# One encoder layer on one core: four edits to what stands where in the engines' queues, and TensorE's order in the last attention stage taken from the program text

## The chip, the cores and the metric

The kernel runs on one core of one Trainium2 chip. The metric is the device time of one launch in microseconds (us). The engines are named as the profile names them: PE is TensorE (matmuls and transposes), DVE is VectorE, ACT is ScalarE, POOL is GpSimd, SP is SyncE, which here only issues DMAs. Each engine works through its own queue in order; an instruction that waits for a semaphore holds up all that stands behind it on that engine.

## What is computed

One layer of a bidirectional encoder on 1024 positions of 1024 channels, in float32: a SwiGLU block, a mixer (Fourier branch and differential attention side by side, gated and merged), a second SwiGLU block, a norm.

```python
x = x + 0.5 * swiglu(rms_norm(x, ffn1_norm[l]), ffn1_wg[l], ffn1_wu[l], ffn1_wd[l])
x = x + hybrid_mixer(rms_norm(x, mix_norm[l]), positions, rel_bias, w_in[l], ...)
x = x + 0.5 * swiglu(rms_norm(x, ffn2_norm[l]), ffn2_wg[l], ffn2_wu[l], ffn2_wd[l])
...
# hybrid_mixer
proj = h @ w_in
u_f, q, k, v, g_a, g_b = jnp.split(proj, cuts, axis=-1)
y_a = fourier_branch(u_f) @ w_fourier_out          # real part of a 2-D DFT, 4 groups of 128 channels
o = diff_attention(q, k, v, positions, rel_bias, lam)   # softmax(s1) - lam * softmax(s2), 4 heads
o = rms_norm(o, subln_g, SUBLN_EPS) * (1.0 - lambda_init)
merged = jax.nn.sigmoid(g_a) * y_a + jax.nn.sigmoid(g_b) * (o.reshape(B, S, V_WIDTH) @ w_attn_out)
return merged @ w_out
```

## The kernel before

**Arithmetic.** Each float32 product is taken as three matmuls on halves: an operand is split into a high part (ACT copies it, L133) and a low part (DVE subtracts, L134), and high·high, high·low and low·high are summed in PSUM. The large products (both SwiGLU blocks, the projection by w_in) go by seven products of 2x2 blocks instead of eight; these are the matmuls of L386, twelve to a product and bank, with ACT (L398) and DVE (L402) taking the products out of PSUM.

**Stages.** SwiGLU 1 runs to about 600 us of the span, the projections with the first two heads of attention beside them to about 1115 us, the last attention stage (heads 2 and 3, with the Fourier branch) to about 1262 us, the product with w_attn_out (L1784, called y_b) and the merge with w_out to about 1470 us, SwiGLU 2 and the last norm to the end.

**What sets the order.** The program is traced once; a scheduler that simulates the engines then sets each engine's order, so an instruction need not stand where the text has it. `in_order(...)` pins one instruction behind everything traced before it on its engine. Side work is written as Python generators (`third`, `hgen`, `fgen`), of which a step is traced at each hook of a main loop.

**What the change touches.**
- `ffn` (SwiGLU 1) works on column pairs j, about 37.5 us each; at its hooks it steps `third`, the generator `mixer_weights` (L746), which prepares the mixer's weights: it loads a piece into an `h` tile (L797 for w_attn_out), some steps later splits it on ACT and DVE (L759, L760, pinned), and stores it as `attn_d` (L802).
- `head_prep(h)` (L1232) prepares a head's operands from `proj_d`: `twice` (L1209) loads a half of q or k into an `rh` tile (two DMAs, L1213; the `rh` ring has three buffers), ACT copies the high part (`q_split` L1221, `k_split` L1229), POOL subtracts the low part (L1222, L1230); then V is loaded (L1248), transposed on PE (L1251) and split. Loads and splits of one step are traced together.
- `fourier` (L1403) is traced in steps from `fill(g, k)`: `tokens(j)` loads a group's token rows (L1427), `fold_tokens` folds them on POOL (L1434 to L1440), PE transposes the fold (L1482), ACT and DVE split it, PE multiplies by the DFT matrix (L1509).
- `fetch_op` (L1622) loads eight pieces of `attn_d`, 512 KB each, for y_b; it issues on SP's queue.
- The last attention stage is the loop over query blocks g = 18 to 33 at L1742: `combine(g-1)` (ACT, POOL L1303: the difference of the two softmaxes), `scores(g, 0)` and `scores(g, 1)` (PE L1285, the two score maps, into tiles A), `fill(g, 0)`, at odd g `weigh(g-3)` (PE L1332, the weights times V), a step of `hgen` (`head_prep(3)`, later norms), `fill(g, 1)`, at odd g `back(g-3)` (PE L1343), `turn(g-1)` (PE L1319, the transposes of the weights). Between scores and turn of a block stand DVE's maximum (L1288), ACT's exponentials (L1291), and `combine`.

## Time and profile before

| | us |
|---|---|
| median of three runs | 2056.62 |
| the three runs | 2057.92, 2055.22, 2056.62 |
| the profiled execution, its own time | 2060.26 |
| its span in the trace | 2058.5 |
| PE busy in it | 1959.3 (95%) |

The span is what the profiler sees between the first and the last instruction; 1.8 us of the execution's time lie around it. A row of the timeline gives start, duration, engine, line, operation, output<-input, how many instructions were merged (x12), and in brackets how long the engine sat idle before it and what ended that idleness. A row of stretches gives, for each engine, its busy time and its instructions in that stretch, then the clock that PE was granted (1.00 is the upper of its two levels, 2.4 GHz), the busy share of the 16 DMA engines and what they moved.

### The profile page before, as it was taken

Reading aid. Unit: us, or ns where it says so; the run is one execution under the profiler, and the core shown is the slowest. Engines: PE = TensorE matmul, PEld = TensorE weight load, DVE = VectorE, ACT = ScalarE, POOL = GpSimd, SP = SyncE. Lnnn points to the kernel's source line nnn. Section 1 sums busy time; section 2 is a strip of 40 time slices with the busy share of each in tenths; the row PEclk is TensorE's granted clock in tenths of the full one; section 3 lists DMA queues with packets and bytes.
Section 4 is the critical chain, followed back from the end, with each engine's and each line's share of the span. In section 5 each row is a group of like instructions: output and inputs, shape, how many; then the busy total and the mean of one; then the engine's idle time right before and its main releaser. Section 6 shows DMA issues by size and latency. Waiting matters only on the chain. (4 is left out here: it accounts for less than half of the span.)

```text
span 2058.5 us, 27602 instructions
## 1 busy us (share of the span) xinstructions
PE 1959.3 (95%) x9433; PEld 1640.7 (80%) x9433; DVE 1417.7 (69%) x2152; ACT 1008.5 (49%) x1814; POOL 652.0 (32%) x487
## 2 busy tenths in 40 slices
PE   4999999999999989999999897997999999999998
PEld 4877878888888888888877786877888888888886
DVE  7877665648767766565666886769665654578765
ACT  6444334334445655778756753256333333344454
POOL 6633323320000364344455650057332323200010
PEclk8899999999999999999999899999999999999999
DMA  4477964418525353344348667421745532256325
GB/s 143 150 251 244 306 223 169 159 57 299 177 87 171 135 167 116 115 141 131 121 152 278 217 205 281 159 103 65 238 166 186 181 110 70 62 201 232 109 96 175
DMA packets 205455, 342.11 MB, mean 166 GB/s; under 512 B 22108, under 2 KB 63052, under 8 KB 204800
## 3 DMA queue, kind: packets, MB, share of 16 engines
q1 hardware_dynamic: 199184, 329.06, 48.1%
q10 hardware_dynamic: 4608, 8.39, 1.1%
q0 software_dynamic: 1520, 2.88, 0.5%
q8 instruction: 74, 1.21, 0.3%
q14 instruction: 69, 0.57, 0.1%
HBM read 250.04 MB, written 94.40 MB: 167 GB/s over the span
## 5 line engine op out<-in xcount | busy, mean ns | idle before, releaser
L386 PE MATMUL p<-n,op 128*128 128x512 f32 (+1 forms) x5256 | 1159.7, 380 | 32.4 <-DVE r L402 9.7
L386 PEld LDWEIGHTS p<-n,op 128*128 128x128 f32 x5256 | 950.1, 192 | 220.7 <-DVE r L402 10.4
L217 POOL TENSOR_TENSOR r<-r,r 128x512 f32<-128x512 f32 x252 | 362.4, 1444 | 877.3 <-DVE op L134 512.7
L134 DVE TENSOR_TENSOR op<-r,op 128x512 fp32r<-128x512 f32 x427 | 358.1, 843 | 279.7 <-ACT op L133 266.3
L133 ACT ACTIVATE op<-r 128x512 fp32r<-128x512 f32 x446 | 277.7, 627 | 286.9 <-PE p L386 197.0
L588 PE MATMUL b<-n 128*128 128x512 f32 x996 | 236.9, 390 | 0.9 <-DVE r L1819 0.9
L588 PEld LDWEIGHTS b<-n 128*128 128x128 f32 x996 | 187.2, 188 | 40.2 <-ACT op L133 1.3
L398 ACT ACTIVATE r<-p 128x512 f32<-128x512 f32 (+1 forms) x138 | 74.1, 537 | 119.0 <-PE p L386 118.6
L588 PE MATMUL b<-op,op 128*128 128x512 f32 x528 | 129.6, 392 | 2.7 <-DVE op L134 2.7
L588 PEld LDWEIGHTS b<-op,op 128*128 128x128 f32 x528 | 99.3, 189 | 23.6 <-DVE op L134 3.1
L402 DVE TENSOR_TENSOR r<-p,r 128x512 f32<-128x512 f32 (+1 forms) x138 | 84.8, 616 | 45.7 <-PE p L386 42.3
L133 ACT ACTIVATE n<-n 128x512 fp32r<-128x512 f32 x126 | 74.7, 621 | 68.1 <-PE b L588 23.3
L134 DVE TENSOR_TENSOR n<-n,n 128x512 fp32r<-128x512 f32 x118 | 83.0, 722 | 30.9 <-ACT n L133 30.9
L588 PE MATMUL p<-n 128*128 128x512 f32 x336 | 80.1, 390 | 0.0
L1878 POOL TENSOR_TENSOR r<-r,x 128x512 f32<-128x512 f32 x5 | 8.0, 1613 | 224.0 <-ACT r L1877 224.0
L588 PEld LDWEIGHTS p<-n 128*128 128x128 f32 x336 | 62.9, 188 | 12.9
L1303 POOL TENSOR_TENSOR x<-x,x 128x1024 f32<-128x1024 f32 x16 | 38.3, 2394 | 104.6 <-ACT x L1302 104.6
L588 PE MATMUL p<-op,op 128*128 128x512 f32 x288 | 68.3, 390 | 0.0
L588 PEld LDWEIGHTS p<-op,op 128*128 128x128 f32 x288 | 53.8, 188 | 11.0
L133 ACT ACTIVATE op<-n 128x512 fp32r<-128x512 f32 x66 | 39.3, 621 | 36.4 <-PE b L588 13.5
L1285 PE MATMUL A<-x,x 128*128 128x512 f32 x144 | 43.7, 404 | 8.3 <-ACT x L1229 6.0
L133 ACT ACTIVATE n<-x 128x512 fp32r<-128x512 f32 x48 | 30.1, 633 | 42.4 <-PE b L588 31.5
(331 smaller groups left out, 2481.3 us busy)
## 6 DMA issues: line engine op xcount, KB each, us to landing
kx<-in_ffn_wd SPq DMA_DIRECT2D x118, 256.0 KB
r<-in_ffn_wg SPq DMA_DIRECT2D x96, 256.0 KB
r<-in_ffn_wu SPq DMA_DIRECT2D x94, 256.0 KB
n<-sums_d SPq DMA_DIRECT2D x88, 256.0 KB
sums_d<-kx SPq DMA_DIRECT2D x66, 256.0 KB
proj_d<-r SPq DMA_DIRECT2D x56, 256.0 KB
h_d<-x SPq DMA_DIRECT2D x16, 512.0 KB
rh<-proj_d SPq DMA_DIRECT2D x64, 128.0 KB
```

The source lines that it names most:

```text
L133: act.activation(hi, src, AF.Copy)
L134: eng.tensor_tensor(out=lo, in0=src, in1=hi, op=ALU.subtract)
L217: pool.tensor_tensor(out=b[o], in0=b[x], in1=b[y], op=op)
L386: pe.matmul(ps, lhsT=w[wi][:, d * P:(d + 1) * P], rhs=xn[b][xi][:, d, cols], start=(first and m == 0), stop=(last and m == 11), skip_group ...
L398: act.activation(o, view(p), AF.Copy)
L402: dve.tensor_tensor(out=o, in0=view(p), in1=o, op=ALU.add)
L588: pe.matmul(ps[p], lhsT=wa[ai][:, p * P:(p + 1) * P], rhs=wb[bi], start=(j == 0 and m == 0 and name in self.FRESH), stop=False, skip_group ...
L1285: pe.matmul(ps[:, ns], lhsT=q[:, qs], rhs=kk[:, ns], start=(n == 0), stop=(n == 1))
L1303: pool.tensor_tensor(out=s1, in0=s2, in1=s1, op=ALU.add)
L1878: pool.tensor_tensor(out=y[1], in0=y[1], in1=gain[1][1], op=ALU.mult)
```

## The change

Four edits move work in the queues, and one takes an order away from the scheduler:
1. `ffn`: `third` is stepped from j = 2 on instead of from j = 1, so each of its loads and splits comes one column pair later.
2. `head_prep`: the loads of a step are traced one hook ahead of their splits; ACT's splits and the first of V's four transposes are pinned.
3. `fourier`: the first POOL copy of a fold and the first of its four transposes are pinned.
4. `fetch_op`: the eight loads are issued on ACT's queue instead of SP's.
5. The last attention loop stands in `tc.manual_schedule(engines={PE})`: in it, PE's order is that of the text; the other engines are still scheduled.

```diff
@@ -904,7 +904,7 @@
                         each()
                         return
                     step(beside)
-                    if third is not None and 1 <= j < SPILL + 4:
+                    if third is not None and 2 <= j < SPILL + 4:
                         step(third)
 
                 seven_products(cols, lambda i, b, c, new=None: evac(i, b, c, new, gate_first), hook,
@@ -1213,20 +1213,18 @@
             sp.dma_start(out=r[half, :], in_=src)
         return r
 
-    def q_split(h, c, hh):
+    def q_split(h, c, hh, r):
 
         hs = slice(hh * HS, (hh + 1) * HS)
-        r = twice(proj_d[h][(L, U)[c], hs])
         q, lo = stk[h][c][:, hs], (U, L)[c]
-        act.activation(q, r, AF.Copy)
+        in_order(act.activation(q, r, AF.Copy))
         pool.tensor_tensor(out=q[lo, :], in0=r[lo, :], in1=q[lo, :], op=ALU.subtract)
 
-    def k_split(h, c, hh):
+    def k_split(h, c, hh, r):
 
         hs = slice(hh * HS, (hh + 1) * HS)
-        r = twice(proj_d[4 + h][(L, U)[c], hs])
         kh, kl = stk[h][2 + c][:, hs], stk[h][4 + c][:, hs]
-        act.activation(kh, r, AF.Copy)
+        in_order(act.activation(kh, r, AF.Copy))
         pool.tensor_tensor(out=kl, in0=r, in1=kh, op=ALU.subtract)
 
     def head_prep(h):
@@ -1237,20 +1235,37 @@
         else:
             stk[h] = [xtile(j, [P, S], F32R) for j in range(5)]
         stk[h].append(T(big, "kx", [P, S], F32R, 2))
-        for fn in (q_split, k_split):
-            for hh in range(2):
-                for c in range(2):
-                    fn(h, c, hh)
-                yield
         vs[h] = [htile(2 * (h == 3) + hh, [P, 4, 2 * P]) for hh in range(2)]
-        for hh in range(2):
+
+        def load_v(hh):
             r = rh()
             sp.dma_start(out=r, in_=proj_d[8 + h][:, hh * HS:(hh + 1) * HS])
+            return r
+
+
+        r = None
+        for fn, t in ((q_split, h), (k_split, 4 + h)):
+            for hh in range(2):
+                if r is not None:
+                    for c in range(2):
+                        due[0](h, c, due[1], r[c])
+                r = [twice(proj_d[t][(L, U)[c], hh * HS:(hh + 1) * HS]) for c in range(2)]
+                due = fn, hh
+                yield
+        for c in range(2):
+            due[0](h, c, due[1], r[c])
+        r = load_v(0)
+        yield
+        for hh in range(2):
             pt = bank()
             for j in range(4):
-                pe.transpose(pt[:, j * P:(j + 1) * P], r[:, j * P:(j + 1) * P], ident)
+                t = pe.transpose(pt[:, j * P:(j + 1) * P], r[:, j * P:(j + 1) * P], ident)
+                if j == 0:
+                    in_order(t)
             p3 = pt.rearrange("p (j c) -> p j c", j=4)
             split(p3, vs[h][hh][:, :, 0:P], vs[h][hh][:, :, P:2 * P])
+            if hh == 0:
+                r = load_v(1)
             yield
 
     sc, dts, ot = {}, {}, {}
@@ -1431,7 +1446,7 @@
 
             even = j < 3
             f, mid = r2(), u[1][:, 0:1]
-            pool.tensor_copy(out=f[:, 0:1], in_=u[0][:, 0:1])
+            in_order(pool.tensor_copy(out=f[:, 0:1], in_=u[0][:, 0:1]))
             pool.tensor_tensor(out=f[:, 1:HS], in0=u[0][:, 1:HS], in1=u[1][:, HS - 1:0:-1],
                                op=ALU.add if even else ALU.subtract)
             g = r2()
@@ -1479,7 +1494,9 @@
             g, quarter = f
             pt = bank("p")
             for k in range(4):
-                pe.transpose(pt[:, k * P:(k + 1) * P], g[:, k * P:(k + 1) * P], ident)
+                t = pe.transpose(pt[:, k * P:(k + 1) * P], g[:, k * P:(k + 1) * P], ident)
+                if k == 0:
+                    in_order(t)
             th, tl = op_split(pt)
             if even:
 
@@ -1619,7 +1636,7 @@
 
     def fetch_op(src):
         o = op_tile()
-        sp.dma_start(out=o.bitcast(F32), in_=src)
+        act.dma_start(out=o.bitcast(F32), in_=src)
         return o[:, 0, :], o[:, 1, :]
 
     for dm in range(DT):
@@ -1739,30 +1756,31 @@
             filled[0] += 1
             step(fgen)
 
-    for g in range(G0 + 2, NG + 2):
-        h, i = divmod(g, TT)
-        if i == 0 and g < NG:
-            if hgen is not None:
-                for _ in hgen:
-                    pass
-            hgen = head_prep(h + 1) if h + 1 < H else early_norms()
-        if g + 2 < NG:
-            get_bias(g + 2)
-        if g - 1 < NG:
-            combine(g - 1)
-        if g < NG:
-            scores(g, 0)
-            scores(g, 1)
-        fill(g, 0)
-        if g % 2 == 1 and G0 + 3 <= g < NG + 1:
-            weigh(g - 3)
-        if g < NG and (i > 0 if h + 1 < H else i > 1):
-            step(hgen)
-        fill(g, 1)
-        if g % 2 == 1 and G0 + 3 <= g < NG + 1:
-            back(g - 3)
-        if g - 1 < NG:
-            turn(g - 1)
+    with tc.manual_schedule(engines={mybir.EngineType.PE}):
+        for g in range(G0 + 2, NG + 2):
+            h, i = divmod(g, TT)
+            if i == 0 and g < NG:
+                if hgen is not None:
+                    for _ in hgen:
+                        pass
+                hgen = head_prep(h + 1) if h + 1 < H else early_norms()
+            if g + 2 < NG:
+                get_bias(g + 2)
+            if g - 1 < NG:
+                combine(g - 1)
+            if g < NG:
+                scores(g, 0)
+                scores(g, 1)
+            fill(g, 0)
+            if g % 2 == 1 and G0 + 3 <= g < NG + 1:
+                weigh(g - 3)
+            if g < NG and (i > 0 if h + 1 < H else i > 1):
+                step(hgen)
+            fill(g, 1)
+            if g % 2 == 1 and G0 + 3 <= g < NG + 1:
+                back(g - 3)
+            if g - 1 < NG:
+                turn(g - 1)
     for _ in fgen:
         pass
     for _ in hgen:
```

What moves is seen in the engines' queues. Names carry a number that tells one buffer or one use from another (A_1347 and A_1348 are the two score maps of g = 19); the changed kernel's lines are shifted by some 15 to 18, so its L1497, L1300, L1334, L1347 are L1482, L1285, L1319, L1332 of before.

PE in the last attention stage, before, around the first transposes of a fold (L1482 into p_1351); A_1407 and A_1408 are the score maps of g = 22, and L1319 turns block 18:

```order
L1285 MATMUL A_1407_11475<-x2_1257_10681,x0_1255_10679 128x512 x2
L1285 MATMUL A_1407_11475<-x4_1259_10683,x0_1255_10679 128x512 x2
L1343 MATMUL b_1364_11242<-ident_63,rh_1358_11209 128x128 x2
L1319 MATMUL b_1369_11252<-ident_63,n2_1308_10946 128x128 x4
L1482 MATMUL p_1351_11163<-ident_63,r2_1350_11158 128x128 x2
L1285 MATMUL A_1408_11482<-x3_1258_10682,x1_1256_10680 128x512 x2
L1285 MATMUL A_1408_11482<-kx_1260_10684,x1_1256_10680 128x512 x2
L1482 MATMUL p_1351_11163<-ident_63,r2_1350_11158 128x128 x2
L1319 MATMUL b_1370_11259<-ident_63,n2_1308_10946 128x128 x4
```

The same place after; A_1327 and A_1328 are the score maps of g = 18, A_1349 and A_1350 those of g = 19, L1334 turns blocks 16 and 17, and L1347 is the first of the weighing of block 16:

```order
L1334 MATMUL b_1322_11049<-ident_63,n0_1302_10905 128x128 x4
L1334 MATMUL b_1323_11056<-ident_63,n0_1302_10905 128x128 x4
L1300 MATMUL A_1328_11082<-x3_1258_10682,x1_1256_10680 128x512 x2
L1300 MATMUL A_1328_11082<-kx_1260_10684,x1_1256_10680 128x512 x2
L1334 MATMUL b_1347_11122<-ident_63,n1_1303_10907 128x128 x4
L1334 MATMUL b_1348_11129<-ident_63,n1_1303_10907 128x128 x4
L1300 MATMUL A_1349_11141<-x2_1257_10681,x0_1255_10679 128x512 x2
L1300 MATMUL A_1349_11141<-x4_1259_10683,x0_1255_10679 128x512 x2
L1300 MATMUL A_1350_11148<-x3_1258_10682,x1_1256_10680 128x512 x2
L1300 MATMUL A_1350_11148<-kx_1260_10684,x1_1256_10680 128x512 x2
L1497 MATMUL p_1353_11163<-ident_63,r2_1352_11158 128x128 x4
L1347 MATMUL b_1359_11184<-n8_1320_11047,h0_1261_10685 128x256
```

The transposes of the first fold now stand behind the scores of g = 19 and ahead of the weighing of block 16; before, they stood behind that weighing and behind the scores of g = 20 and 21 and half of those of g = 22.

ACT before, at the splits of head 2 (L1221 for q, L1229 for k) between the evacuations (L398) and splits (L133) of the projections:

```order
L133 ACTIVATE op_1284_10786<-r2_1227_10509 128x512
L1364 ACTIVATE rh_1245_10600<-b_1244_10583 128x128
L1221 ACTIVATE x0_1255_10679<-rh_1261_10685 128x512
L398 ACTIVATE r2_1277_10768<-p_1254_10666 128x512
L133 ACTIVATE op_1289_10814<-r2_1239_10559 128x512
L1221 ACTIVATE x1_1256_10680<-rh_1262_10690 128x512
L133 ACTIVATE op_1294_10842<-r2_1268_10726 128x512
L1221 ACTIVATE x0_1255_10679<-rh_1266_10714 128x512
L1221 ACTIVATE x1_1256_10680<-rh_1267_10719 128x512
L133 ACTIVATE op_1297_10868<-r2_1271_10734 128x512
L1229 ACTIVATE x2_1257_10681<-rh_1275_10758 128x512
```

ACT after, the same splits (L1220, L1227):

```order
L398 ACTIVATE r2_1290_10810<-p_1287_10787 128x512
L133 ACTIVATE op_1293_10835<-r2_1270_10724 128x512
L1220 ACTIVATE x0_1255_10679<-rh_1263_10687 128x512
L1220 ACTIVATE x1_1256_10680<-rh_1264_10690 128x512
L133 ACTIVATE op_1296_10861<-r2_1273_10732 128x512
L1220 ACTIVATE x0_1255_10679<-rh_1268_10716 128x512
L1220 ACTIVATE x1_1256_10680<-rh_1269_10719 128x512
L1227 ACTIVATE x2_1257_10681<-rh_1277_10760 128x512
L1175 ACTIVATE r2_1298_10883<-p_1254_10666 128x512
```

The first split now stands behind the evacuation and the split of a later product, and no evacuation stands between the four splits of q.

SP before, at the loads for y_b (L1622) behind the loads of the merge (L146), of SwiGLU 2's rows (L489) and of stored sums (L505):

```order
L146 DMA r2_1632_12747<-ya_d_85 128x512
L146 DMA r2_1633_12749<-proj_d_84 128x512
L146 DMA r2_1635_12766<-ya_d_85 128x512
L146 DMA r2_1636_12768<-proj_d_84 128x512
L489 DMA h2_1661_12964<-x1_d_82 128x512 x2
L489 DMA h3_1662_12965<-x1_d_82 128x512 x2
L505 DMA n9_1613_12677<-sumso_d_76 128x512
L505 DMA n8_1612_12676<-sumso_d_76 128x512
L1622 DMA op_1631_12731<-attn_d_77 128x1024
L1622 DMA op_1638_12771<-attn_d_77 128x1024
```

ACT after, at the end of the attention stage; L1410 is the last scaling of head 3's output, which y_b waits for, and L133 behind are splits for w_out:

```order
L1410 ACTIVATE x6_1599_12604<-b_1610_12670,sgain_7914 128x512
L1639 DMA op_1631_12734<-attn_d_77 128x1024
L1639 DMA op_1638_12774<-attn_d_77 128x1024
L1639 DMA op_1647_12814<-attn_d_77 128x1024
L1639 DMA op_1650_12846<-attn_d_77 128x1024
L133 ACTIVATE n12_1644_12810<-n9_1613_12680 128x512
```

The four loads moved from behind the row of loads on SP to a place on ACT right behind the last scaling.

## Rows read from the trace of the kernel before

**Rows 1.** The page: busy time, share of the span and instructions of each engine.

```profile
PE 1959.3 (95%) x9433; PEld 1640.7 (80%) x9433; DVE 1417.7 (69%) x2152; ACT 1008.5 (49%) x1814; POOL 652.0 (32%) x487
```

**Rows 2.** Busy time by stretch: us, engines, clock, DMA share, GB/s.

```profile
225.00:250.00 25.00, 25.00 (x112) 20.67 (x112) 15.37 (x22) 10.32 (x18) 3.94 (x3) 1.00 0.97 332
250.00:275.00 25.00, 21.74 (x88) 17.12 (x87) 19.06 (x20) 8.19 (x14) 11.91 (x8) 0.93 0.59 206
1100.00:1130.00 30.00, 27.42 (x143) 22.66 (x141) 22.81 (x45) 22.83 (x39) 13.36 (x16) 1.00 0.99 314
1130.00:1262.00 132.00, 122.61 (x726) 105.02 (x724) 102.01 (x217) 76.99 (x147) 64.64 (x58) 0.95 0.63 206
1262.00:1290.00 28.00, 18.53 (x70) 14.11 (x69) 20.85 (x38) 6.02 (x12) 0.00 (x0) 0.82 1.04 386
```

**Rows 3.** Timeline, SP, ACT and PE at 261 to 270 us (SwiGLU 1).

```profile
261.34 0.77 SPq L797 DMA_DIRECT2D h<-in_w_attn_out  x1
...
265.76 0.63 ACT L759 ACTIVATE h<-h 128x512 fp32r<-128x512 f32 x1 [2.23 <-DMA h<-in_w_attn_out]
...
266.93 3.27 PE L386 MATMUL p<-n,op 128*128 128x512 f32 x7 [3.26 <-ACT x L398]
```

**Rows 4.** Timeline, ACT and PE at 766 to 772 us (head 1's splits).

```profile
766.02 0.63 ACT L1229 ACTIVATE x<-rh 128x512 fp32r<-128x512 f32 x1 [1.98 <-DMA rh<-proj_d]
...
766.79 0.47 PE L1285 MATMUL A<-x,x 128*128 128x512 f32 x1 [1.73 <-ACT x L1229]
...
767.18 4.58 PE L386 MATMUL p<-n,op 128*128 128x512 f32 x12
```

**Rows 5.** Timeline, ACT and PE at 1081 to 1090 us (head 2's splits).

```profile
1081.15 0.63 ACT L1229 ACTIVATE x<-rh 128x512 fp32r<-128x512 f32 x1 [1.76 <-DMA rh<-proj_d]
...
1081.92 0.47 PE L1285 MATMUL A<-x,x 128*128 128x512 f32 x1 [4.27 <-ACT x L1229]
...
1082.32 4.61 PE L386 MATMUL p<-n,op 128*128 128x512 f32 x12
...
1086.99 2.89 PE L386 MATMUL p<-n,op 128*128 128x512 f32 x12
```

**Rows 6.** Timeline, SP, POOL and PE at 1115 to 1153 us (first folds).

```profile
1115.05 0.34 SPq L1460 DMA_DIRECT2D n<-cx_d  x1
...
1116.54 3.80 SPq L1427 DMA_DIRECT2D r<-proj_d  x1
...
1117.49 2.39 POOL L1303 TENSOR_TENSOR n<-n 128x1024 f32<-128x1024 f32 x1 [2.48 <-ACT n L1302]
...
1126.11 0.19 POOL L1434 COPY r<-r 128x1 f32<-128x1 f32 x1 [6.23 <-DMA r<-proj_d]
...
1127.50 1.26 POOL L1435 TENSOR_TENSOR r<-r,r 128x511 f32<-128x511 f32 x1 [1.20 <-DMA r<-proj_d]
...
1129.03 1.41 POOL L1440 TENSOR_TENSOR r<-r 128x255 f32<-128x255 f32 x2
...
1117.50 0.60 PE L1319 MATMUL b<-ident,n 128*128 128x128 f32 x4
...
1129.80 0.44 PE L1482 MATMUL p<-ident,r 128*128 128x128 f32 x2 [2.27 <-POOL r L1440]
...
1152.12 1.38 PE L1482 MATMUL p<-ident,r 128*128 128x128 f32 x4 [2.72 <-POOL r L1440]
```

**Rows 7.** Timeline, PE and SP at 1272 to 1293 us (y_b).

```profile
1272.68 1.07 PE L1784 MATMUL A<-x,op 128*128 128x512 f32 x4
...
1273.59 2.29 SPq L489 DMA_DIRECT2D h<-x_d  x4
...
1277.62 1.66 SPq L1622 DMA_DIRECT2D op<-attn_d  x3
...
1284.17 2.90 PE L1784 MATMUL b<-x,op 128*128 128x512 f32 x6 [6.80 <-DMA op<-attn_d]
...
1291.10 1.52 PE L1784 MATMUL b<-x,op 128*128 128x512 f32 x6
```

## The prediction

> **What bounds the kernel now.** I read the page first. PE is busy for 1959.3 us [rows 1] of the 2058.5 us span, so what can be won lies in PE's 99 us of idle time, and in matmuls that run at the lower clock. Then I read PE's timeline from start to end for every idle stretch with its releaser, and for each the timelines of the engine that ended it. Much of the idleness is out of the change's reach: the start of the kernel, the norms behind the merge, and everything from 1470 us on, where PE runs without a gap. Four gaps and one stage are within reach: the gaps at 266.93, 766.79, 1081.92 and 1284.17 us [rows 3, 4, 5, 7], and the attention stage up to 1262 us, in which PE idles for 9.4 us after 1130 (132.00 less 122.61) at a mean granted clock of 0.95 [rows 2].
>
> A gap costs more than its length. After the 1.73 us gap the next twelve matmuls of L386 take 4.58 us [rows 4], after the 4.27 us gap 4.61; the same twelve a few us on take 2.89 [rows 5]. That is 1.7 us more each time: after PE has stood still, some of its matmuls run at 1.2 GHz. The stretch with the gap at 266.93 has a granted clock of 0.93, the one before it 1.00 [rows 2]. So gaps of about 1.7 us and more are charged some 1.7 us on top.
>
> **The change part by part, against the profiled execution.**
>
> *Part 1, `third` a column pair later.* ACT sits for 2.23 us on L759, which waits for a load that SP issued at 261.34, only 4.4 us before L759 began at 265.76; PE's next matmuls need the evacuation right behind it and stand still for 3.26 us [rows 3]. The cause lies further back: the DMA engines were 0.97 busy from 225 to 250 us [rows 2], so loads and POOL's and DVE's work were late. That stretch holds 112 matmuls at full clock (0.223 us each), the next one 88 [rows 2]: 24 x 0.223 = 5.4 us lost. With the change the splits at this place belong to an earlier piece of work relative to their loads; in ACT's new order the split that reads this load stands some 8 to 14 instructions later, about 10 us, which covers 2.23 us several times. Moved with it are the loads L797 and stores L802 on SP and the pinned pair on DVE; they come no oftener than before, and with a DMA share of 0.59 after 250 us [rows 2] there is room for them. Bounds: 5.4 us if the gap goes, 0 if POOL's late work makes the same hole one instruction on. I take 4.5.
>
> *Part 2, loads of `head_prep` a hook ahead.* At head 1 ACT waits 1.98 us on L1229 for `rh`, and PE 1.73 us on that [rows 4]; with the slower matmuls after it (4.58 - 2.89 = 1.7) 3.4 us. At head 2 ACT waits 1.76 us in the last of a chain of such waits and PE 4.27 us, with 1.7 us behind: 6.0 us [rows 5]. With the change the loads are issued one hook earlier, and the splits and the first score matmul stand about two products later in ACT's and PE's order; a product is twelve matmuls, 2.89 us [rows 5], so about 5.8 us are gained against 4.27. What may take the gap's place: `rh` has three buffers and a step needs two, so the second load of a step still waits for a split of the step before, and a pinned split that waits for its load now holds up the evacuations (L398) behind it as before. Bounds: 9.4 us for both, and 0. I take 2.5 and 4.5, 7.0 together. V's pinned transposes and the POOL subtracts go along; I cost them at nothing, since PE has projection matmuls on both sides. Without that cover each pin would cost a wait of the order of 1 to 2 us.
>
> *Part 4, y_b's loads on ACT's queue.* PE's longest gap in the reach of the change, 6.80 us, ends when a load of `op` lands; the first six matmuls after it take 2.90 us instead of 1.52 [rows 7]. SP issues these loads at 1277.62, behind four loads from 1273.59 on and others [rows 7]. The buffer was free earlier: PE's last reads of the first one end about 1273.6 [rows 7]. ACT has nothing ahead of the loads then, so they can be issued some 4.0 us sooner (1277.62 - 1273.6), and the landing with them. The splits that stand behind the four loads on ACT are for w_out, 25 us later, so ACT's wait is free; if it were not, it would cost up to the 4 us that it sits there. The gap does not vanish: issue at 1273.6 and the 6.55 us from issue to PE's start (1284.17 - 1277.62) give 1280.2, still 2.8 us of idleness and the slow matmuls. Against it speaks the load of the DMA engines, which move 386 GB/s between 1262 and 1290 us [rows 2]: an earlier issue then shares the same bandwidth with what SP issues at the time. Bounds: 0 and 4.0. I take 3.5.
> The Trainium skill ("Trainium Kernel Development and Optimization", section Key Constraints) says that DMAs issued from SP, ACT and POOL all run on the same 16 DMA engines and interleave, so that issuing from several engines saves only the sequencer's issue time. By that rule alone this term is the 2.3 us in which SP issues the four loads ahead [rows 7], and the sum 1.2 us poorer; no row here shows the same load from both queues.
>
> *Parts 3 and 5, PE in program order.* This is the part that may cost. In the text the transposes of the first fold (L1482) follow the scores of g = 19; in the order before they came behind the weighing of block 16 and the scores of two and a half more blocks. So PE reaches them at about 1118.6 us: the turn before them ended at 1118.1 [rows 6], and about 0.5 us of the other turn is left. Before, PE had worked until 1127.53 (1129.80 less 2.27) [rows 6]; about 8.9 us of work moves behind the transposes. When can they start? The fold's token rows are loaded at 1116.54 on SP, with 3.80 us in the issue itself, behind a load of 1115.05 that waits for the last projection matmuls; POOL waits for them 6.23 and 1.20 us and starts L1435 at 1127.50; with L1440 the fold is done about 1130.4 [rows 6]. The DMA engines are 0.99 busy from 1100 to 1130 us [rows 2], and nothing in the change brings the rows in much earlier: I allow 1.5 us, because the last projection product now ends a little sooner relative to this work. On POOL, in the new order, a `combine` (L1303, 2.39 us [rows 6]) stands between L1435 and L1440, so the transposes start at about 1131 (1130.4 - 1.5 + 2.4, less a little as L1303 is ready early). PE stands still from 1118.6 to 1131, over 12 us instead of 2.27.
> Compared with before, PE at 1131 is 8.9 + 1.2 = 10 us of work behind. Against that stands what the wait gives back: while PE waits, ACT, DVE and POOL finish what later blocks need, and a block's PE work, 122.61 us [rows 2] over 16 blocks or 7.7 us, is longer than its chain through maximum, exponentials and `combine`, which I estimate at 7 us with L1303's 2.39 as its longest member. Of the 9.4 us that PE idles after 1130, and some 3 us of slow matmuls there (0.05 of 122.61 at half speed would be 6; I count half), I expect 5 us to stay: the chain at the end of the stage, and a wait like the one at 1152.12 (2.72 us [rows 6]). So 10 - 4.4 - 0.6 = 5 us are lost. Bounds: a gain of 9 if the token rows land with PE's arrival, a loss of 15 if every fold is met too early as the first.
>
> **The sum.** -4.5 - 7.0 - 3.5 + 5 = -10 us: 2050.3 us on the profiled execution's 2060.26. That execution is 3.64 us above the median of the runs, so the forecast for the median is 2046.6, say 2047.
>
> **The rivals.**
> (a) *PE stalls at the folds, and the change is slower.* PE in text order stands at L1482 for a fold that depends on token rows, a POOL copy pinned behind `combine`, and ACT's and DVE's split. If the wait is 12 us at the first fold and 2.72 at each of the next four with 1.7 us of slow matmuls each, the stage loses 10 + 4 x 4.4 - 9.4 = 18 us; the gaps of parts 1, 2, 4 give 15 at best and perhaps 8, so 2060 to 2067. It decides from the point where the stage's loss exceeds the sum of the gaps that go. For it: POOL is the engine that ended both L1482 waits [rows 6], and the text puts no other work there. Against it: later folds are loaded and folded two or more blocks ahead.
> (b) *The stage gains too.* If the tokens come in time, the stage loses its 9.4 us of idleness, less the last chain, and the sum is -15 - 6 = -21: 2036. For it: the text interleaves evenly. Against it: POOL's 6.23 us wait for the rows [rows 6].
> (c) *The gaps move instead of going.* L759 meets another late load, the three `rh` buffers hold the splits back as before, and y_b's loads land no sooner. Then parts 1, 2 and 4 give some 5 us, and the stage takes them: 2054 to 2059, no change. For it: the loads are late because DMA engines are at 0.97 [rows 2], and no part moves fewer bytes.
>
> **How the numbers follow.** A difference of 0.2% (4.1 us) is about what a measurement of this kernel can tell from no change. The forecast's case, a gain of 5 to 15 us, has 0.45; (b) 0.15; (c) 0.20; (a) 0.20. So faster 0.60, same 0.20, slower 0.20. The range takes in (b) and (c) and the lower part of (a): 2036 to 2062. The forecast's own range is 2041 to 2052.
>
> **What would show it.** Part 1: no gap of PE near 267 us, and over 100 matmuls of L386 between 250 and 275. Part 2: the score matmuls after L1229 begin without idleness, and no L386 x12 of 4.6 us. Part 4: the gap in y_b about 2.8 us. Parts 3 and 5: a gap of some 10 us at the first L1482 and hardly any in the 30 us after it. The forecast is wrong if that gap is below 5 us (then it is too high), if there is one like it at each fold, or if the gaps at 267, 767 and 1082 us stand as before (then it is too low).

## The result, and the profile after

The changed kernel takes 2086.28 us (median of 2081.19 to 2093.06), the kernel before 2056.72 (2055.22 to 2057.92), four runs each: a ratio of 1.0137, 95% interval [1.0116, 1.0157]. It is slower by some 29 us; 2047 with a range to 2062 was predicted. The profiled execution took 2088.43 us, 28.2 more than the one of before. The page of the kernel after, in the row that answers to [rows 1]:

```profile
PE 1967.4 (94%) x9433; PEld 1647.9 (79%) x9433; DVE 1423.0 (68%) x2152; ACT 1003.0 (48%) x1808; POOL 650.9 (31%) x487
```

Where the time went is read by laying points of PE's timeline side by side:

| point on PE | before | after | after - before |
|---|---|---|---|
| first turn (L1319) of the last attention stage | 1112.00 | 1105.36 | -6.6 |
| y_b's first matmuls on head 3 (L1784) | 1262.99 | 1293.33 | +30.3 |
| y_b goes on behind its load | 1284.17 | 1311.61 | +27.4 |
| first matmul with w_out (L588) | 1308.52 | 1337.46 | +28.9 |
| span | 2058.5 | 2086.7 | +28.2 |

Up to the attention stage the change gained 6.6 us. The stage itself, 150.99 us long before, is 187.97 long after: 37.0 us lost in one place. Behind it little moves. (PE's order differs, so the point is not the same amount of work in both: at the first turn PE has done eight matmuls more after than before. At 0.223 us each that makes the gain up to there an estimated 8.4 us and the loss in the stage 38.8.)

Busy time by stretch after (us, then PE, PEld, DVE, ACT, POOL with instructions, PE's granted clock, DMA share, GB/s); the first two stretches answer to those of [rows 2], the third is the attention stage:

```profile
225.00:250.00 25.00, 24.42 (x108) 19.89 (x107) 14.98 (x21) 9.16 (x16) 4.02 (x3) 1.00 0.99 333
250.00:275.00 25.00, 24.68 (x108) 19.81 (x107) 22.72 (x26) 10.58 (x19) 11.02 (x8) 1.00 0.69 251
1105.40:1292.80 187.40, 147.51 (x807) 125.15 (x805) 121.90 (x246) 94.80 (x175) 68.31 (x66) 0.87 0.53 175
```

The same stage of the kernel before, from its first turn to y_b:

```profile
1112.00:1262.70 150.70, 138.68 (x815) 117.99 (x813) 115.03 (x242) 92.14 (x172) 72.59 (x68) 0.95 0.68 222
```

The gap near 267 us is gone: 108 matmuls between 250 and 275 us instead of 88, with the clock at 1.00 instead of 0.93. In the stage nearly the same work (807 and 815 matmuls) takes PE 147.5 us busy instead of 138.7, at a mean clock of 0.87 instead of 0.95, and around it PE stands still for 39.9 us (187.40 - 147.51) instead of 12.0 (150.70 - 138.68). So of the 36.7 us between the two windows, 27.9 are idleness and 8.8 longer busy time.

What PE waited for in the stage, after (tile and line that waited, what ended the wait: us in all, times, longest):

```profile
PE p L1497 <- POOL r L1454: 17.8, 2, 9.3
PE p L1526 <- ACT op L133: 3.9, 2, 3.2
PE b L1334 <- DVE oss L1366: 2.8, 3, 1.3
PE b L1334 <- DVE n L134: 2.8, 2, 1.8
```

and before:

```profile
PE p L1482 <- POOL r L1440: 5.0, 2, 2.7
PE A L1285 <- DVE nms L1288: 2.6, 4, 1.4
```

Waits for folds (L1497 after, L1482 before) grew by 12.8 us. The rest of the idleness, waits of 0.3 to 3.2 us at turns and at the Fourier matmuls (L1526), grew by 15.1 (39.9 - 17.8 less 12.0 - 5.0).

PE at the folds, after; 1110.82 is the last score of g = 19, L1526 multiplies a transposed fold:

```profile
1110.82 0.62 PE L1300 MATMUL A<-kx,x 128*128 128x512 f32 x2
1120.73 1.12 PE L1497 MATMUL p<-ident,r 128*128 128x128 f32 x4 [9.29 <-POOL r L1454]
...
1149.23 1.11 PE L1497 MATMUL p<-ident,r 128*128 128x128 f32 x4 [8.51 <-POOL r L1454]
...
1164.94 0.79 PE L1526 MATMUL p<-n,op 128*128 128x256 f32 x2 [3.22 <-ACT op L133]
1167.94 2.50 PE L1526 MATMUL p<-n,op 128*128 128x256 f32 x10 [2.21 <-DVE op L134]
```

POOL over the same time (L1450, L1449, L1455, L1454 are the fold, in the order in which POOL has them; L1318 is a combine, L1228 a head's low parts):

```profile
1113.38 1.27 POOL L1450 TENSOR_TENSOR r<-r,r 128x511 f32<-128x511 f32 x1 [10.23 <-DMA r<-proj_d]
1116.13 2.90 POOL L1318 TENSOR_TENSOR n<-n 128x1024 f32<-128x1024 f32 x1 [1.48 <-ACT n L1317]
1118.98 0.18 POOL L1449 COPY r<-r 128x1 f32<-128x1 f32 x1
1119.12 1.40 POOL L1455 TENSOR_TENSOR r<-r 128x255 f32<-128x255 f32 x2
1120.48 0.34 POOL L1454 TENSOR_TENSOR r<-r,r 128x1 f32<-128x1 f32 x2
...
1139.32 1.28 POOL L1450 TENSOR_TENSOR r<-r,r 128x511 f32<-128x511 f32 x1 [2.94 <-DVE nms L1303]
1141.72 2.92 POOL L1318 TENSOR_TENSOR n<-n 128x1024 f32<-128x1024 f32 x1 [1.11 <-ACT n L1317]
1144.59 0.64 POOL L1449 COPY r<-r 128x1 f32<-128x1 f32 x1
1145.19 1.40 POOL L1455 TENSOR_TENSOR r<-r 128x255 f32<-128x255 f32 x2
1146.55 1.25 POOL L1228 TENSOR_TENSOR x<-rh,n 128x512 fp32r<-128x512 f32 x1
1147.77 1.25 POOL L1228 TENSOR_TENSOR kx<-rh,n 128x512 fp32r<-128x512 f32 x1
1148.99 0.33 POOL L1454 TENSOR_TENSOR r<-r,r 128x1 f32<-128x1 f32 x2
```

PE reached the first transposes at 1111.4 and stood for 9.29 us. Of these the token rows account for the time to 1113.38, when L1450 starts; then POOL waits for a combine's input and runs it (1116.13, 2.90) before it may go on with the fold, since the pinned copy L1449 stands behind that combine. At the third fold the same: L1450 starts at 1139.32, a combine and two head splits stand between the fold's own instructions, and the fold ends at 1149.3.

At the heads' splits, PE, DVE and POOL after; they answer to [rows 4, 5]:

```profile
774.40 0.66 PE L1262 MATMUL b<-ident,rh 128*128 128x128 f32 x4 [1.50 <-DMA rh<-proj_d]
...
1077.54 0.47 PE L1300 MATMUL A<-x,x 128*128 128x512 f32 x1 [1.12 <-ACT x L1227]
...
1085.41 4.15 PE L386 MATMUL p<-n,op 128*128 128x512 f32 x10 [3.78 <-DVE op L134]
...
1079.36 6.00 DVE L134 TENSOR_TENSOR op<-r,op 128x512 fp32r<-128x512 f32 x1 [7.65 <-ACT op L133]
...
1083.55 1.25 POOL L1228 TENSOR_TENSOR x<-rh,x 128x512 fp32r<-128x512 f32 x1
```

The gaps at L1229 did go, and others stand near where they were: at head 1 PE now waits 1.50 us for V's load instead of 1.73, and at head 2, 1.12 us for a split and 3.78 us for DVE's L134, 4.9 us for 4.27. That L134 had its high part from ACT and began at 1079.36, but it took 6.00 us. POOL worked from 1076.14 to 1084.80 without a pause, in turn at the heads' low parts and at other subtracts, and DVE's L134 ended 0.56 us behind the last of them. Before, POOL paused at this head for ACT's splits (1.71 us ahead of its row at 1081.91), and the L134 that began at 1079.42 took 1.33 us.

y_b's loads, ACT and PE, after; they answer to [rows 7]:

```profile
1298.71 0.69 ACT L1410 ACTIVATE x<-b,sgain 128x512 fp32r<-128x512 f32 x1 [3.68 <-PE b L1407]
1305.57 5.66 ACTq L1639 DMA_DIRECT2D op<-attn_d  x4
...
1311.61 2.90 PE L1802 MATMUL b<-x,op 128*128 128x512 f32 x6 [3.72 <-DMA op<-attn_d]
```

ACT has finished with L1410 at 1299.4 and issues the loads at 1305.57; PE's gap is 3.72 us.

### The profile page after: what moved, and what is told of

It reads as the page before. It is cut to its first block, busy times and chain, and to the rows that moved or that the text cites. A ratio compares the mean times of both kernels' runs of the same rounds, so it can differ in the third digit from the quotient of the medians.

```text
span 2086.7 us, 27577 instructions
## 1 busy us (share of the span) xinstructions
PE 1967.4 (94%) x9433; PEld 1647.9 (79%) x9433; DVE 1423.0 (68%) x2152; ACT 1003.0 (48%) x1808; POOL 650.9 (31%) x487
## 5 line engine op out<-in xcount | busy, mean ns | idle before, releaser
L386 PE MATMUL p<-n,op 128*128 128x512 f32 (+1 forms) x5256 | 1154.3, 379 | 31.7 <-DVE r L402 8.3
L386 PEld LDWEIGHTS p<-n,op 128*128 128x128 f32 x5256 | 947.4, 191 | 218.7 <-DVE op L134 8.2
L134 DVE TENSOR_TENSOR op<-r,op 128x512 fp32r<-128x512 f32 x427 | 360.1, 848 | 286.4 <-ACT op L133 269.4
L133 ACT ACTIVATE op<-r 128x512 fp32r<-128x512 f32 x446 | 277.6, 627 | 293.0 <-PE p L386 205.0
L588 PE MATMUL b<-n 128*128 128x512 f32 x996 | 237.1, 391 | 0.9 <-DVE r L1837 0.9
L588 PEld LDWEIGHTS b<-n 128*128 128x128 f32 x996 | 187.1, 188 | 40.1 <-ACT op L133 1.3
L398 ACT ACTIVATE r<-p 128x512 f32<-128x512 f32 (+1 forms) x138 | 74.1, 537 | 128.3 <-PE p L386 128.1
L588 PE MATMUL b<-op,op 128*128 128x512 f32 x528 | 129.5, 392 | 2.7 <-DVE op L134 2.7
L588 PEld LDWEIGHTS b<-op,op 128*128 128x128 f32 x528 | 99.5, 189 | 23.8 <-DVE op L134 3.1
L402 DVE TENSOR_TENSOR r<-p,r 128x512 f32<-128x512 f32 (+1 forms) x138 | 84.6, 615 | 40.8 <-PE p L386 38.8
L133 ACT ACTIVATE n<-n 128x512 fp32r<-128x512 f32 x126 | 74.7, 621 | 75.5 <-PE b L588 23.3
L134 DVE TENSOR_TENSOR n<-n,n 128x512 fp32r<-128x512 f32 x118 | 81.5, 708 | 34.3 <-ACT n L133 34.2
L588 PE MATMUL p<-n 128*128 128x512 f32 x336 | 80.1, 390 | 0.0
L588 PEld LDWEIGHTS p<-n 128*128 128x128 f32 x336 | 62.9, 188 | 12.9
L1318 POOL TENSOR_TENSOR x<-x,x 128x1024 f32<-128x1024 f32 x16 | 38.4, 2398 | 103.7 <-ACT x L1317 103.7
L588 PE MATMUL p<-op,op 128*128 128x512 f32 x288 | 68.3, 391 | 0.0
L588 PEld LDWEIGHTS p<-op,op 128*128 128x128 f32 x288 | 53.8, 188 | 11.0
L133 ACT ACTIVATE op<-n 128x512 fp32r<-128x512 f32 x66 | 39.3, 621 | 35.7 <-PE b L588 13.9
L1303 DVE CUSTOM_DVE_ANT_0 x<-A,x 128x1024 f32<-128x1024 f32 x32 | 39.0, 1218 | 21.3 <-PE b L1334 11.0
L133 ACT ACTIVATE n<-x 128x512 fp32r<-128x512 f32 x48 | 30.1, 632 | 45.2 <-PE b L588 31.5
```

What stands on the lines that cost most here:

```text
L133: act.activation(hi, src, AF.Copy)
L134: eng.tensor_tensor(out=lo, in0=src, in1=hi, op=ALU.subtract)
L386: pe.matmul(ps, lhsT=w[wi][:, d * P:(d + 1) * P], rhs=xn[b][xi][:, d, cols], start=(first and m == 0), stop=(last and m == 11), skip_group ...
L398: act.activation(o, view(p), AF.Copy)
L402: dve.tensor_tensor(out=o, in0=view(p), in1=o, op=ALU.add)
L588: pe.matmul(ps[p], lhsT=wa[ai][:, p * P:(p + 1) * P], rhs=wb[bi], start=(j == 0 and m == 0 and name in self.FRESH), stop=False, skip_group ...
```

## Experiments

Theory T: PE in text order meets results (folds above all) before they are made; parts 1, 2 and 4 give back about what the table shows. Rival P: the pins of parts 2 and 3 hold up ACT and POOL whatever PE's order is. The first four runs tell them apart.

**e1_no_text_order**: parts 1 to 4.

```diff
-    with tc.manual_schedule(engines={mybir.EngineType.PE}):
+    if True:
```

> The changed kernel without its fifth part: PE's order in the last attention stage is again the scheduler's, parts 1 to 4 stay. Theory T (PE in text order meets the folds before POOL has made them, and the stage loses some 37 us of which parts 1, 2 and 4 give 9 back): the stage is again about as long as before, the gap near 267 us stays away, and the time is 2046 to 2052 us. Rival P (the pins of parts 2 and 3 alone hold up ACT and POOL, whatever PE's order): most of the loss stays, 2070 to 2085 us.

Measured: 2055.29 us, ratio 0.9984 [0.997, 0.9998]; the stage is 152.6 us long. T holds in its main point: without the fifth part the loss is gone. But the time lies above the 2046 to 2052 that T gave: parts 1 to 4 together gain only about 3 us (0.4 to 6 by the interval), and not the 9 of the table. In this order the pins cost too. DVE, ACT and PE in the stage:

```profile
1144.87 4.33 DVE L134 TENSOR_TENSOR x<-r,x 128x512 fp32r<-128x512 f32 x1
...
1149.67 0.40 ACT L1537 ACTIVATE r<-p 128x256 f32<-128x256 f32 x1 [7.72 <-issue]
...
1151.06 0.69 PE L1358 MATMUL b<-ident,rh 128*128 128x128 f32 x2 [7.71 <-ACT rh L1350]
```

ACT stands 7.7 us ahead of L1537, and PE waits 7.71 for L1350 behind it. The profile names no releaser for L1537; it starts 0.08 us after the end of DVE's L1535, which stands behind the L134 of 4.33 us. POOL, in whose order the pinned folds stand, worked nearly without a pause from 1138.50 to 1148.65, and that L134 ended 0.55 us later, as in the trace of after.

**e2_text_order_alone**: the fifth part on the kernel before.

```diff
+    with tc.manual_schedule(engines={mybir.EngineType.PE}):
...
     for g in range(G0 + 2, NG + 2):
```

> The kernel before with the fifth part alone: PE's order in the last attention stage is the text's, no pins, no moved loads. Theory T: PE stands at the first transposes of a fold for some 9 us and at the third for several, and the stage loses 20 to 35 us: 2077 to 2092 us. Rival P (the loss needs the POOL pin): the stage loses under 10 us, 2057 to 2066.

Measured: 2083.26 us, ratio 1.0128 [1.0103, 1.0153]; the stage is 180.17 us long, 36.35 of it idle. As T expected: this part alone costs some 26 us, and P falls as the main cause. PE's two longest waits in it:

```profile
1129.63 1.37 PE L1482 MATMUL p<-ident,r 128*128 128x128 f32 x4 [7.50 <-POOL r L1440]
...
1154.22 1.97 PE L1319 MATMUL b<-ident,n 128*128 128x128 f32 x8 [4.38 <-POOL n L1303]
```

The first fold again, and at 1154.22 a turn that stands ahead of POOL's combine.

**e3_no_pool_pin**: the changed kernel without the pin on the fold's copy.

```diff
-            in_order(pool.tensor_copy(out=f[:, 0:1], in_=u[0][:, 0:1]))
+            pool.tensor_copy(out=f[:, 0:1], in_=u[0][:, 0:1])
```

> The changed kernel with the pin on the fold's first POOL copy taken away; PE stays in text order. In POOL's order the fold then stands ahead of the combine that it stood behind. Theory T: the waits at the first and the third fold's transposes shrink from 9.3 and 8.5 us to about 5 and 3 and the time falls by 8 to 14 us, to 2072 to 2078; the rest of the loss stays with PE's order. If the pin is all of it, 2045 to 2055; if it is none of it, 2084 to 2088.

Measured: 2075.96 us, ratio 1.0092 [1.0065, 1.0118]; the waits at the first and the third fold are 4.23 and 2.74. As T expected: some 10 us of the loss are the POOL pin on top of text order.

**e4_fold_a_step_ahead**: one more step between a fold and its transposes.

```diff
-FOURIER_STEPS = 40
+FOURIER_STEPS = 45
...
             g, quarter = f
+            yield
             pt = bank("p")
```

> The changed kernel with one more step of the Fourier generator between each fold and its transposes (45 steps instead of 40, spread over the same blocks), so that in the text PE has the weighing or the next scores between them; the pins and the text order stay. Theory T: PE no longer waits 9.3 and 8.5 us at the transposes, two thirds of these waits and the slow matmuls behind them go, and the time falls by 12 to 20 us, to 2066 to 2074. If the loss does not come from the place of the transposes, it stays within 4 us of 2086.

Measured: 2073.08 us, ratio 1.0077 [1.0057, 1.0096]. As T expected, at the upper end: the place of the transposes in the text costs some 13 us. No wait in the stage is over 3 us any more, and still PE is idle for 30.9.

**e9_fold_ahead_no_pool_pin**: e3 and e4 together.

> The changed kernel with both edits: no pin on the fold's POOL copy, and one more step of the Fourier generator between each fold and its transposes. Each alone took 10 and 13 us off. If PE's loss in text order were all waiting for folds, both together give 2052 to 2060 us. If the two edits take away the same waits, the time stays at 2068 to 2074, and what is left are the many waits of 1 to 3 us for splits, turns and combines that the text puts close behind what they depend on.

Measured: 2077.12 us, ratio 1.0086 [1.0066, 1.0106]; stage 173.25 us, 29.39 idle. This is above the 2068 to 2074 that was given for edits that take away the same waits, and no better than e3 or e4 alone; far from the 2052 to 2060 that was given if folds were all of the loss. Some of what PE waited for in the stage:

```profile
PE b L1334 <- DVE oss L1366: 5.1, 6, 1.5
PE p L1527 <- ACT op L133: 5.0, 3, 3.5
PE p L1498 <- POOL r L1455: 3.0, 2, 1.7
```

Folds are down to 3.0 us; 26 us of idleness have nothing to do with them. So the folds are about a third of the stage's loss, not its whole.

**e12_back_a_block_later**: e9, with `back` moved away from the turns.

```diff
+            if g % 2 == 0 and G0 + 4 <= g:
+                back(g - 4)
             if g < NG:
                 scores(g, 0)
...
-            if g % 2 == 1 and G0 + 3 <= g < NG + 1:
-                back(g - 3)
             if g - 1 < NG:
                 turn(g - 1)
```

> The run with fold ahead and no POOL pin, still in text order, with back (L1358) moved from the end of an odd block, where it stands directly ahead of the two turns, to the start of the next block ahead of its scores. The two PSUM banks named b are written by weigh, back and turn in the text's order, and PE waited 5.1 us for DVE's L1366, which reads back's bank, and some 8 us more at the turns and at back. Theory B (what is left of the loss is uses of the same two banks standing side by side): these waits shrink by 4 to 8 us and the time falls from 2077 to 2067 to 2073 us. If the place of back does not matter, it stays within 4 us of 2077.

Measured: 2070.76 us, ratio 1.0075 [1.0052, 1.0098]. The median is 6.4 us below e9's, as theory B said, but the two ratios differ by 0.0011 only, some 2 us, and their intervals overlap; the stage is 2.7 us shorter (170.52) and as idle as e9's (29.5). What PE waited for most:

```profile
PE b L1358 <- DVE n L134: 5.3, 5, 1.6
PE b L1407 <- DVE rh L1404: 5.1, 2, 4.5
```

The wait for L1366 is gone, and `back` itself now waits for the other user of its bank (DVE L134). That neighbours in the text share two PSUM banks names one of the waits that are left. What it costs is not shown: the waits moved, and the sum of idleness stayed.

The next four runs take one of the other parts each, on the kernel before.

**e5_third_alone**: `1 <= j` becomes `2 <= j`.

> The kernel before with part 1 alone (the weights' generator a column pair later). Theory G (the gap near 267 us goes and nothing takes its place): PE is 5 to 6 us ahead by 450 us and the time falls by as much, to a ratio of 0.997 to 0.998. Rival (the lead is given back at a later wait that was hidden so far): PE is ahead by 450 us and level at the end, ratio 0.999 to 1.001.

Measured: 2050.13 us, ratio 0.9958 [0.9944, 0.9972], 8.6 us faster (5.8 to 11.5 by the interval). Theory G in its place, and more than the 5 to 6 us that it gave. PE is 5.4 us ahead from 350 us on, 6.0 where it waits for DVE's L402 (746.43 against 752.45) and 9.3 at the first turn of the attention stage (1102.70 against 1112.00). Not all of that lead is part 1's: the traces of e7 and e8, which lack it, are 2.0 and 4.3 us ahead at that turn too, since the traced execution of before took 3.64 us more than its median.

**e6_head_loads_alone**: `head_prep`, `q_split` and `k_split` of the change.

> The kernel before with part 2 alone (loads of a head's operands a hook ahead of pinned splits). As predicted, the gaps near 767 and 1082 us go: 7 us less, ratio 0.9965. Rival M (they move: the pinned splits now hold up ACT's splits for the projections behind them, and PE waits for DVE's operand instead; V's transposes wait for their load): gaps of 1.5 us near 775 and of some 5 us in all near 1080 to 1088 stand in their place, and the time stays within 2 us, ratio 0.999 to 1.001.

Measured: 2059.26 us, ratio 1.0002 [0.9991, 1.0014]. Rival M: the gaps moved. At 779.95 PE waits 1.32 us for V's load, at 1088.64 it waits 3.48 us for DVE's L134, and the ten matmuls behind that take 4.64 us. It is the picture of after, though not for the reason that the expectation gave: ACT released that L134 at 1082.89, and it took 5.69 us, until 0.55 us after POOL's row of subtracts had ended at 1088.03.

**e7_queue_alone**: `sp.dma_start` becomes `act.dma_start` in `fetch_op`.

> The kernel before with part 4 alone (y_b's loads on ACT's queue). As predicted, the loads start 4 us sooner and the 6.8 us gap shrinks to some 3: ratio 0.998 to 0.9985. Rival S (the DMA engines are the limit there, so the loads land hardly sooner): the gap stays over 5 us, ratio 0.999 to 1.001.

Measured: 2063.58 us, ratio 1.0023 [1.0012, 1.0033], slower. ACT and PE at y_b:

```profile
1274.80 0.63 ACT L133 ACTIVATE n<-n 128x512 fp32r<-128x512 f32 x1 [4.26 <-DMA n<-in_w_out]
1279.59 5.81 ACTq L1622 DMA_DIRECT2D op<-attn_d  x4
...
1285.60 2.47 PE L1784 MATMUL b<-x,op 128*128 128x512 f32 x5 [7.59 <-DMA op<-attn_d]
```

ACT is free from 1275.4 on and the loads leave at 1279.59, no sooner behind the last head scaling than SP issued them (10.4 us after the start of the last L1392 in both). The gap is 7.59 us, longer than the 6.80 of [rows 7]. Rival S, and a loss that neither side expected. Most of that loss lies elsewhere: from the first turn to y_b it is 154.95 us instead of 150.99, with as many matmuls and a wait that before does not have:

```profile
1179.44 1.22 PE L1544 MATMUL p<-x,r 128*128 128x512 f32 x2 [3.47 <-DMA r<-in_dft_chan]
```

POOL issues that load (a DFT matrix) at 1170.04, behind a combine; before, at 1168.10, ahead of the combine. Its second piece also landed 8.75 us after the issue instead of 4.73; why is not shown.

**e8_pins_alone**: the two pins of part 3.

> The kernel before with part 3 alone (the fold's first POOL copy and the first of its transposes pinned, PE's order otherwise the scheduler's). As predicted, without text order it costs nothing: ratio 0.999 to 1.001. Rival P (the POOL pin puts the fold behind a combine, so folds end later and ACT or PE wait for them in the attention stage): 3 to 8 us more, ratio 1.0015 to 1.004.

Measured: 2061.59 us, ratio 1.0015 [1.0005, 1.0025]: 3 us slower. Rival P at its low end. In its stage PE waits 4.62 us at 1146.31 for the split of a transposed fold, which on DVE stands behind an L134 of 3.13 us (1139.57), run while POOL worked without a pause.

The four parts alone sum to -8.6 + 0 + 4.9 + 3 = about -1 us; together (e1) they gave -3.

The last two ask what y_b's load waits for.

**e10_third_pinned_loads**: part 1, and the merge's later loads pinned behind y_b's.

```diff
+    def pinned(src):
+        r = r2()
+        in_order(sp.dma_start(out=r, in_=src))
+        return r
...
-        while len(ready) < min(n_ + 9, len(todo)):
-            ready.append(inputs(*todo[len(ready)]))
+        while len(ready) < min(n_ + 5, len(todo)):
+            ready.append(inputs(*todo[len(ready)], pinned))
```

> The kernel before with part 1, and on SP's queue the loads that the merge needs later (16 of 256 KB) pinned behind y_b's loads and looked ahead for 5 pieces instead of 9: of them two instead of fourteen are then issued ahead of y_b's next load. Theory D (that load waits for the DMA engines, which move what was issued before it): the 6.8 us gap in y_b shrinks to under 3 us, and the time falls below part 1 alone by 4 to 8 us, ratio 0.992 to 0.994. Rival B (it waits for its buffer, which PE frees only at the end): the gap stays at 5 us or more, ratio 0.995 to 0.997.

Measured: 2045.69 us, ratio 0.9948 [0.9934, 0.9961]: faster than before, and the fastest median of all, 4.4 us below part 1 alone, though the two intervals overlap and the ratio is just above the 0.992 to 0.994 of theory D. SP and PE, then the stretch that answers to the last of [rows 2]:

```profile
1258.00 0.98 SPq L505 DMA_DIRECT2D n<-sumso_d  x2
1266.91 0.32 SPq L1622 DMA_DIRECT2D op<-attn_d  x1
...
1260.65 1.08 PE L1392 MATMUL b<-ident,rh 128*128 128x128 f32 x4 [5.90 <-DVE rh L1389]
...
1262.00:1290.00 28.00, 28.00 (x120) 22.85 (x119) 25.16 (x42) 5.59 (x10) 0.00 (x0) 0.97 0.82 295
```

Theory D as to the gap, which is gone: the load leaves at 1266.91, as soon as PE's last reads of its buffer are over and 6.3 us after the last L1392 started instead of 10.4, and PE is busy for all of the 28 us from 1262 to 1290 (18.53 before); the engines move 295 GB/s instead of 386. Part of it is given back: the last head scaling waits 5.90 us instead of 2.27, since DVE's chain to it now stands behind a split that waits for a load of w_out.

**e11_third_pinned_loads_queue**: the same with part 4.

> The same as the run with pinned loads, but y_b's loads on ACT's queue (part 4), so that SP's pins no longer hold back the fourteen loads, which go to the same DMA engines at the same time. Theory D: the gap in y_b is again 5 to 8 us and the gain of the pinned loads is gone, ratio 0.996 to 0.999. If ACT's queue had DMA time of its own, the gap would be as short as on SP's queue, ratio 0.992 to 0.994.

Measured: 2055.25 us, ratio 0.9991 [0.9982, 1.0], 9.6 us above e10. The time is what theory D gave, and the reason is not. On ACT's queue the fourteen loads go out beside y_b's, and the DMA share from 1252 to 1280 us is 1.03 instead of 0.81. But the gap that D put at 5 to 8 us is 2.14, and most of the loss stands in the attention stage, 157.70 us long instead of e10's 150.79, with the wait that e7 has too:

```profile
1174.29 1.22 PE L1544 MATMUL p<-x,r 128*128 128x512 f32 x2 [4.67 <-DMA r<-in_dft_chan]
...
1281.13 1.63 PE L1784 MATMUL b<-x,op 128*128 128x512 f32 x6 [2.14 <-DVE n L1824]
```

Here, as in e10, the last L1392 came late itself (it waited 5.06 us); y_b's load left at 1275.02, 6.9 us after it and as soon as PE's last reads of the buffer were over, although the fourteen loads had gone ahead. This run therefore does not decide between the queue and the bytes ahead of the load; before, e7 and e10 do.

## Why the prediction was wrong

- **The step that failed: "a block's PE work ... is longer than its chain", so 5 us of waiting would stay behind the first fold.** The first gap itself came out near the forecast: over 12 us forecast, 9.29 seen, with the token rows earlier than thought (POOL began at 1113.38) and the combine in between as described. But the term of the whole stage was +5 and measured +37: PE stood still for 39.9 us there and not for the first gap and some 5 more. The bound "a loss of 15" does not follow from its own condition, since five folds met as early as the first, at 10 us each, would lose some 50; and the 0.6 in "10 - 4.4 - 0.6" comes from no row. The two lengths, 7.7 us and an estimated 7, are not what the runs refute; what failed is the step from them to "I expect 5 us to stay". A block's chain fits beside a block's work only if each consumer stands far from its producer; the text puts transposes, split and matmuls of a fold, and `back` and two turns on two banks, one behind the other. e9 shows that folds are not the whole: with their waits down to 3.0 us, 26 us of idleness stay, where before, outside the folds, there were 7.0. Which of the other neighbourhoods costs how much stays open (e12 moved the waits and not their sum). The scheduler's order was worth some 26 us here (e2), and the prediction put no price on its many odd interleavings ([rows 6] show transposes in two halves with scores between).
- **Rival (a) named the right place and sign** and had 0.20; its price of 18 us counted folds alone. e9 shows the rest beside it.
- **Part 1** was right in place and too small in size: -4.5 was taken, -8.6 measured (e5, 5.8 to 11.5). 5.4 us stand from 350 us on, which is the upper bound that the prediction gave; where the rest arises is not shown.
- **Part 2**: -7.0 was taken, 0 measured (e6). The step that failed is "V's pinned transposes and the POOL subtracts go along; I cost them at nothing". The waits at L1229 that the term was made of did go. But with its inputs ready POOL then ran its row without a pause, and beside it one subtract on DVE, the low part that PE needed next, took 5.69 us (e6) and 6.00 us (after) instead of 1.33. PE waited 3.48 and 3.78 us for it, and V's transposes for their load another 1.3 to 1.5. The danger that was listed, a pinned split that holds up ACT, is not what these waits come from. All seven traces with part 2 have one such subtract, of 5.69 to 6.03 us, and none of the seven without it has one over 3.13. That POOL's row is the reason is read from these rows; no run kept the loads ahead and spaced POOL's work.
- **Part 4**: -3.5 was taken, +4.9 measured (e7). The buffer was free when the prediction said, and in e7 ACT was free at 1275.4; what failed is the step from there to an earlier issue. The load left ACT's queue at 1279.59, 0.08 us after a load of `ya_d` that SP had issued at 1274.11 had landed. From SP's queue it also left 0.06 us behind such a landing: 1277.62 after 1277.56 before, 1267.16 after 1267.10 in e5. So from either queue the issue stood until an earlier load had landed (that the two are tied is read from these times), and the 386 GB/s that the prediction named against itself [rows 2] are what those loads share. With two loads ahead instead of fourteen it left as soon as PE freed the buffer (e10). The Trainium skill's rule ("Trainium Kernel Development and Optimization", section Key Constraints: the queues of SP, ACT and POOL share the same 16 DMA engines, and several of them save issue time only) agrees with before and e7, where the load is equally late from both queues; even the 2.3 us of issue time were not gained. At y_b the move cost 0.8 us of gap (7.59 for 6.80), in the attention stage 4.0, with a wait of 3.47 us for the DFT matrix whose late landing is not explained.
- **Part 3** has no price of its own in the prediction and costs 3 us without text order (e8): the pinned fold lengthens POOL's row, and a DVE subtract beside it took 3.13 us (e8) and 4.33 us (e1).
- The forecast of 2047 is thus wrong by sign: -15 of gains were -1 to -3, +5 of loss was 26 (e2) to 31 (after against e1).

## What to carry to other kernels

Before taking an order away from a scheduler, go down the new order and ask of every instruction how much work stands between it and what it waits for, buffers and PSUM banks included; one long wait is easily seen, and twenty short ones cost more. When work is moved or pinned, look at what runs beside it on the other engines too: here a row of POOL's subtracts without a pause came with a DVE subtract of 4 to 6 us that PE was waiting for. When a gap ends with a DMA, ask first what its issue waited for, the queue, the buffer or the landing of earlier loads; another queue helps only with the first.

## What the runs showed of the hardware

The charge of 1.7 us for slower matmuls behind a gap is not fixed. After the same wait in the same place, the twelve matmuls of L386 took 4.58 us in the trace of before [rows 4], at a granted clock of 0.62, and 3.06 in that of e7, at 1.00, with PE's order the same up to there:

```profile
767.12 0.47 PE L1285 MATMUL A<-x,x 128*128 128x512 f32 x1 [1.79 <-ACT x L1229]
767.52 3.06 PE L386 MATMUL p<-n,op 128*128 128x512 f32 x12
```

3.04 stand there in e8, 3.02 in e5 and 3.00 in e10, after 1.86, 1.44 and 1.51 us, at a clock of 1.00. Between 1070 and 1090 us each of the fourteen traces has a gap of 3.0 to 4.3 us. Behind it the twelve matmuls took 4.05 to 4.61 us in the seven traces where the gap stands ahead of twelve, and the ten took 3.86 to 4.64 us in six of the seven where it stands ahead of ten; in the seventh, e4, they took 2.58 us after a gap of 3.02, at a clock of 1.00. So the slow matmuls followed a gap of 1.4 to 1.9 us in one trace of five, and one of 3.0 to 4.3 us in thirteen of fourteen. Over the stage after, with its many gaps, the mean clock was 0.87, and 0.95 before.

A subtract on DVE can take several times its usual time beside a busy POOL. In the trace of before, 706 of the 918 L134 on 128x512 ran with POOL idle (under 5% of their time beside it), and none of them took over 0.71 us; those that ran beside POOL took up to 2.68. In each of the seven traces with part 2 one took 5.69 to 6.03 us, and in e1 another 4.33; in after, e6 and e1, where the rows were read, each of these ended 0.55 or 0.56 us after the end of a row that POOL had worked off without a pause or nearly so.
